# RWKV decays and learning rates: made per unit of 128 tokens, or per block of 512 tokens from split operands and passed through DRAM

## The chip, the cores and the metric

One core of a Trainium2 chip runs the whole kernel. The metric is the device time of one execution in microseconds. The engines are TensorE (PE in the profile, its weight loads PEld), VectorE (DVE), ScalarE (ACT), GpSimd (POOL) and SyncE (SP), which issues every DMA of this kernel, in order. A timed run of the kernel before took 2934.18 us in the median.

## The reference

A decoder layer over 2048 tokens of width 1024: a mixer (gated linear attention, GLA, beside an RWKV-7 group) and a gated MLP. The change concerns two small products of the RWKV group, low-rank ("LoRA") maps from 64 to 512 columns:

```
p = p + (token_shift(p) - p) * mu
w_log = -softplus(-(w0 + tanh(p[..., c0:c1]) @ w_up)) - 0.5
decay = exp(-exp(w_log))
a = sigmoid(a0 + p[..., c1:c2] @ a_up)
k = k * (1 + (a - 1) * k_a)
y = wkv7_scan(r, decay, k, v, -kk, kk * a)
```

Here c0:c1 and c1:c2 are 64 columns each of the projection. The kernel uses sigmoid(z) = (1 + tanh(z/2)) / 2, so the logarithm of the decay is -exp(-0.5) times a sigmoid.

## The kernel before, in words

Tokens are cut into 4 blocks of 512 (NB). `stage_b(b)` projects block b: per 128 output columns 24 products of 128x512 into one PSUM bank (`gemm3`: operands split into a high and a low fp32r part, three products for each of 8 slices of the depth). There are two such banks (`gbank`, tag "g"). `evacuate` empties a bank with ACT, mixes in the token before (DVE, POOL) and stores the result by DMA to DRAM (`pd`); it goes through tiles named ev, a ring of three (`nev`). Column tile TWA holds the 64 decay columns and the 64 rate columns on 128 partitions; it comes before TPG and the 12 tiles of r, k and v.

The weights of the projections (`Weights`) come in pieces of 128x512. In block 0 a piece is loaded into w_st (ring of 4), split into w_hi and w_lo (ring of 6 each, `nhl`) and the two parts are stored to DRAM (khi, klo); later blocks load the parts back.

The recurrences work in units of 128 tokens, 16 in all. For each unit, `rwkv_p` prepares the operands, `rwkv_i` and `rwkv_j` invert a small triangular matrix, `rwkv_s` does the state steps and `gla` the attention chunk. In `rwkv_p` (lines 770 to 808) a unit loads its 128 columns of TWA as rw_wa (L776), takes tanh of the first 64 partitions (L792), makes eight fp32 products of depth 64 into two rp banks (L797 decays, L798 rates), finishes them with tanh on ACT (L800, L803), a scaling on POOL (L801, L805) and the factor of k on DVE (L804), and runs the prefix sum of the log decays (L808).

A list scheduler fixes the order of every engine's instructions when the kernel is built. Between steps of a unit `fill` emits, at a lower priority, the next steps of the projection of the following block: while block b's units run, `stage_b(b+1)` is the filler. `boundary` empties the filler before the first unit of a block is prepared. Block 0's projection is emitted alone, ahead of all units; only the first two GLA chunks overlap with it.

Of the kernel before, what the change touches and what calls it, by code (L numbers as in the profile page):

```python
# [95 lines left out]
def hybrid_kernel(ctx, tc, x, cst, vec, c_row, ada_t, w_in, w_v, w_first, w_z, gk_up, wa_up, g_up,  # L96
# [18 lines left out]
    def gbank():  # L115
        return pools["psum"].tile([P, 512], F32, name="g_bank", tag="g", bufs=pools["g"])
# [11 lines left out]
    def vcol(name, k=0, n=1):  # L128
        o, w = _VL[name]
        return vt[:, o + k:o + k + n]  # L130
# [5 lines left out]


    proj = [[None] * NPROJ for _ in range(NBLK)]
    groups = ((TQ, 2), (TK, 2), (TV, 4), (TG, 4), (TZ, 1), (TR, 4), (TRK, 4), (TRV, 4), (TWA, 1), (TPG, 1))
    pd = [{t0: dram.tile([P, n, NB], F32, name=f"proj_{b}_{t0}") for t0, n in groups} for b in range(NBLK)]  # L140
    mixd = [dram.tile([P, 8, NB], F32, name=f"mix_{b}") for b in range(NBLK)]
    x2d = [dram.tile([P, KT, NB], F32, name=f"x2_{b}") for b in range(NBLK)]

# [11 lines left out]
        return ct[:, o - P:o - P + w]  # L155

    pools["w"] = ph1.enter_context(tc.tile_pool(name="wp1", bufs=2))
    pools["np"], pools["nst"], pools["nhl"], pools["nev"], pools["nx"] = 2, 4, 6, 3, 2
    pools["h"] = ph1.enter_context(tc.tile_pool(name="hp1", bufs=1))
    pools["hb"] = 9  # L160

# [131 lines left out]
    def dst_of(b, t):  # L293
        for t0, n in groups:
            if t0 <= t < t0 + n:
                return pd[b][t0][:, t - t0, :]
# [25 lines left out]
    def stage_a(b, ks):  # L322
# [2 lines left out]
            ahead[b] = (spread(ap, ahead[b]), [])  # L325
        modulate(ap, src, ahead[b][0], 0, ks, ahead[b][1])

    def evacuate(b, t, ps):
        ev = ap.tile([P, NB], F32, name="ev", tag="ev", bufs=pools["nev"])
        if t < TZ:  # L330
            A.activation(out=ev, in_=ps, func=AF.Copy, scale=0.125 if t < TK else 1.0)
        else:

            m = t - TR
            A.activation(out=ev, in_=ps, func=AF.Copy, scale=omu[:, m:m + 1])
            V.scalar_tensor_tensor(out=ev[:, 1:NB], in0=ps[:, 0:NB - 1], scalar=vcol("mu", m), in1=ev[:, 1:NB], op0=ALU.mult, op1=ALU.add)
            G.tensor_tensor(out=ev[:, 0:1], in0=ev[:, 0:1], in1=carry[:, m:m + 1], op=ALU.add)
            A.activation(out=carry[:, m:m + 1], in_=ps[:, NB - 1:NB], func=AF.Copy, scale=vcol("mu", m))
        nc.sync.dma_start(out=dst_of(b, t), in_=ev)

    def values_tok(b, h, i):
# [21 lines left out]
    def stage_b(b):  # L363

        h = ahead.pop(b)[1]
        order = ([TZ] + list(range(8, TZ)) if b == 0 else list(range(8)) + [TZ] + list(range(8, TZ))) + [TWA, TPG] + [TR + i for i in range(12)]
        for i_, t in enumerate(order):
            if b + 1 < NBLK:
                if i_ == len(order) - 15:
                    ahead[b + 1] = stats_a(b + 1)  # L370
                if i_ == len(order) - 11:
                    stats_b(b + 1)
                if i_ == len(order) - 7:
                    stage_a(b + 1, range(0, EXTRA))
                if i_ == len(order) - 2:
                    stage_a(b + 1, range(EXTRA, KT))
            if t == TZ:

                ps = gbank()
                w = Weights(w_z, split=False, cols=KT * 32)  # L380
                for i in range(2):
                    for p_ in range(2):
                        for j in range(4):
                            k = 4 * i + j
                            PE.matmul(out=ps[32 * j:32 * j + 32], lhsT=w.cut(w.st, k * 32, 32), rhs=h[k][p_].bitcast(F32),
                                      start=i == 0 and p_ == 0, stop=i == 1 and p_ == 1)
                ev = ap.tile([P, NB], F32, name="ev", tag="ev", bufs=pools["nev"])
                A.activation(out=ev, in_=ps, func=AF.Identity, bias=vcol("zone"))
                nc.sync.dma_start(out=pd[b][TZ][:, 0, :], in_=ev)
                yield  # L390
                continue
            if TV <= t < TG:
                if (t - TV) % 2 == 0:
                    yield from values_tok(b, h, (t - TV) // 2)
                continue
            if b > 0 and i_ < 2:
                if i_ == 0:
                    bks = pair_gemm(w_in, 0, "in", h, b + 1 < NBLK)
                ps = bks[i_]
            elif b + 1 < NBLK and i_ >= len(order) - 2:  # L400
                if i_ == len(order) - 2:
                    bks = pair_gemm(w_in, t - 1, "in", h, b + 1 < NBLK)
                ps = bks[i_ - len(order) + 2]
            else:
                ps = gbank()
                t_ = t if t < TZ else t - 1
                gemm3(ps, Weights(w_in[t_], key=("in", t_), keep=b + 1 < NBLK), h)
            evacuate(b, t, ps)
            yield

    filler, lag = [None], [370]
    rate, due = [0.85], [0.0]
# [177 lines left out]
    ahead[0] = (rb, h0)  # L590
    nc.sync.dma_start(out=ct, in_=cst[:, P:c0])

    wa_up = cst1([P, 512], "wa_up", wa_up)
    g_up_sb = cst1([P, 512], "g_up_sb", g_up)
    gk_up_sb = cst1([P, 256], "gk_up_sb", gk_up)
    wlev = cst1([P, 1152], "wlev", dt=F32R)
# [173 lines left out]
    def rwkv_p(b, q, n):  # L770
        cs = slice(q * CQ, (q + 1) * CQ)
        K, R = qp("rw_k"), qp("rw_r")
        VV = ctile([P, 4, CQ], F32, name="rw_v", tag="rw_v", bufs=1)
        wa = ctile([P, CQ], F32, name="rw_wa", tag="rw_wa", bufs=1)
        pg = ctile([P, CQ], F32, name="rw_pg", tag="rw_pg", bufs=2)
        nc.sync.dma_start(out=wa, in_=pd[b][TWA][:, 0, cs])  # L776
        nc.sync.dma_start(out=K, in_=pd[b][TRK][:, :, cs])
        nc.sync.dma_start(out=R, in_=pd[b][TR][:, :, cs])
        nc.sync.dma_start(out=VV, in_=pd[b][TRV][:, :, cs])
# [9 lines left out]
        V.scalar_tensor_tensor(out=vc, in0=vm.unsqueeze(2).broadcast_to([P, 8, 64]), scalar=-1.0 / 64.0, in1=pv, op0=ALU.mult, op1=ALU.add)  # L789

        lw, an, kp_ = qp("rw_lw"), qp("rw_an"), qp("rw_kp")
        A.activation(out=wa[0:64], in_=wa[0:64], func=AF.Tanh)  # L792
        psw, psa = bank("rp"), bank("rp")
        pw_ = psw.rearrange("p (j t) -> p j t", j=4)
        pv = psa.rearrange("p (j t) -> p j t", j=4)
        for j in range(4):
            PE.matmul(out=pw_[:, j, :], lhsT=wa_up[0:64, j * P:(j + 1) * P], rhs=wa[0:64, :], start=True, stop=True)  # L797
            PE.matmul(out=pv[:, j, :], lhsT=wa_up[64:128, j * P:(j + 1) * P], rhs=wa[64:128, :], start=True, stop=True)  # L798
        for j in range(4):
            A.activation(out=lw[:, j], in_=pw_[:, j], func=AF.Tanh, scale=0.5, bias=w0h[:, j:j + 1])  # L800
        G.tensor_scalar(out=lw, in0=lw, scalar1=-0.5 * DECAY, scalar2=-0.5 * DECAY, op0=ALU.mult, op1=ALU.add)  # L801
        for j in range(4):
            A.activation(out=an[:, j], in_=pv[:, j], func=AF.Tanh, scale=0.5, bias=a0h[:, j:j + 1])  # L803
            V.tensor_scalar(out=kp_[:, j], in0=an[:, j], scalar1=kah[:, j:j + 1], scalar2=kah[:, 4 + j:5 + j], op0=ALU.mult, op1=ALU.add)  # L804
        G.tensor_scalar(out=an, in0=an, scalar1=-0.5, scalar2=-0.5, op0=ALU.mult, op1=ALU.add)  # L805
        for i in range(2):
            lwc = lw[:, 2 * i:2 * i + 2].rearrange("p j t -> p (j t)")
            V.tensor_tensor_scan(out=lwc, data0=cc("m64"), data1=lwc, initial=0.0, op0=ALU.mult, op1=ALU.add)  # L808
# [762 lines left out]
```

## Time and profile before

| what | value |
|---|---|
| timed runs, median (lowest to highest of 3) | 2934.18 us (2933.49 to 2939.03) |
| profiled execution, its own time | 2927.03 us |
| span of its trace | 2925.2 us |
| PE, DVE, ACT, POOL busy, share of the span | 94%, 71%, 44%, 37% |
| DMA moved | 486.91 MB, 166 GB/s over the span |

Times in the profile are microseconds from the start of the span unless marked ns. A row of a matmul gives the time from its start until its result is out, so successive matmuls overlap: their pace is read from start to start. An fp32 product is recorded as two instructions. The column after "<-" names what ended an engine's idle time.

### The profile page before, as it was taken

The numbers are of one execution on the slowest core, as the hardware profiler recorded it, in microseconds if no ns is written. First come the engines' busy times: TensorE is split into PE (matmuls) and PEld (weight loads), VectorE is DVE, ScalarE is ACT, GpSimd is POOL, SyncE is SP. The second block draws the span as 40 slices with busy tenths as digits, with TensorE's granted clock in tenths as the row PEclk, the third lists the DMA queues.
The fourth block names the chain that finished last, engine by engine and source line by source line (L and its number), as shares of the span: only waits on it lengthen the run. The fifth ranks groups of instructions, "written<-read, shape, count | busy, mean of one in ns | idle before, by whom it ended". The sixth has DMA issues, their size and how long they took to land.

```text
span 2925.2 us, 54728 instructions
## 1 busy us (share of the span) xinstructions
PE 2751.4 (94%) x20296; PEld 2229.9 (76%) x20296; DVE 2085.8 (71%) x4103; ACT 1298.4 (44%) x2721; POOL 1088.3 (37%) x1150
## 2 busy tenths in 40 slices
PE   6989999999999999999779999999997999999998
PEld 5767777877787777778557888888776788888887
DVE  8356977656676667886687685776868786685867
ACT  4444345444444446443354353442534444353443
POOL 5213222312221223332456363553436454363541
PEclk9999999999999999889789999999998999999999
DMA  8989945645545566546314425234564624425243
GB/s 287 352 288 312 280 139 178 191 143 159 171 150 154 163 196 206 164 124 213 120 43 162 141 87 166 87 126 149 185 227 144 209 94 129 138 90 162 88 130 110
DMA packets 363532, 486.91 MB, mean 166 GB/s; under 512 B 80769, under 2 KB 153729, under 8 KB 363265
## 3 DMA queue, kind: packets, MB, share of 16 engines
q1 hardware_dynamic: 363264, 483.41, 51.9%
q8 instruction: 160, 2.62, 0.4%
q14 instruction: 108, 0.88, 0.1%
HBM read 342.77 MB, written 140.51 MB: 165 GB/s over the span
## 4 chain that ended last, share of the span: by engine, by line
PE 69%; DVE 13%; DMA 9%; ACT 3%; issue 3%; POOL 2%; SPq 0%; DVEq 0%; POOLq 0%; ACTq 0%
PE g_bank L1270 9%; PE g_bank L1268 9%; PE g_bank L1269 9%; PE g_bank L1325 5%; PE g_bank L1327 5%; PE g_bank L1326 5%; PE g_bank L281 4%; PE g_bank L283 4%; PE g_bank L282 4%; PE gl_bank L698 1%; DMA rw_k<-proj 1%; DMA acc<-acc 1%; PE g_bank L450 1%; DMA w_st<-in_ada_t 1%; PE g_bank L452 1%
## 5 line engine op out<-in xcount | busy, mean ns | idle before, releaser
L1268 PE MATMUL g_bank<-h_hi,w_hi 128*128 128x512 f32 x1232 | 488.0, 396 | 26.6 <-ACT h_hi L1143 14.8
L1269 PE MATMUL g_bank<-h_lo,w_hi 128*128 128x512 f32 x1232 | 487.3, 396 | 12.7 <-DVE h_lo L1165 6.8
L1270 PE MATMUL g_bank<-h_hi,w_lo 128*128 128x512 f32 x1232 | 479.7, 395 | 9.7 <-POOL w_lo L1144 7.8
L1143 ACT CAST w_hi<-w_st 128x512 fp32r<-128x512 f32 (+1 forms) x396 | 238.6, 607 | 487.4 <-PE g_bank L1326 348.4
L1328 DVE SCALAR_TENSOR_TENSOR acc<-g_bank,mod,acc 128x512 f32<-128x512 f32 (+1 forms) x200 | 144.7, 728 | 249.7 <-PE g_bank L1327 230.7
L1144 POOL TENSOR_TENSOR w_lo<-w_st,w_hi 128x512 fp32r<-128x512 f32 x154 | 219.3, 1425 | 241.7 <-ACT w_hi L1143 237.9
L281 PE MATMUL g_bank<-h_hi,w_hi 128*128 128x512 f32 x736 | 299.0, 406 | 8.0 <-DMA w_hi<-khi 3.8
L1268 PEld LDWEIGHTS g_bank<-h_hi,w_hi 128*128 128x128 f32 x1232 | 235.1, 191 | 81.6 <-ACT h_hi L1143 18.0
L282 PE MATMUL g_bank<-h_lo,w_hi 128*128 128x512 f32 x736 | 294.9, 401 | 0.0
L283 PE MATMUL g_bank<-h_hi,w_lo 128*128 128x512 f32 x736 | 294.9, 401 | 0.0
L1269 PEld LDWEIGHTS g_bank<-h_lo,w_hi 128*128 128x128 f32 x1232 | 235.0, 191 | 64.1 <-DVE h_lo L1165 8.2
L1270 PEld LDWEIGHTS g_bank<-h_hi,w_lo 128*128 128x128 f32 x1232 | 234.9, 191 | 63.3 <-POOL w_lo L1144 12.3
L1325 PE MATMUL g_bank<-hh,w_hi 128*128 128x512 f32 x640 | 251.9, 396 | 6.0 <-DVE acc L1328 6.0
L1326 PE MATMUL g_bank<-hl,w_hi 128*128 128x512 f32 x640 | 251.6, 395 | 0.0
L1327 PE MATMUL g_bank<-hh,w_lo 128*128 128x512 f32 x640 | 251.6, 395 | 0.0
L1144 DVE TENSOR_TENSOR w_lo<-w_st,w_hi 128x512 fp32r<-128x512 f32 (+1 forms) x242 | 201.6, 833 | 15.2 <-ACT w_hi L1143 10.5
L281 PEld LDWEIGHTS g_bank<-h_hi,w_hi 128*128 128x128 f32 x736 | 140.3, 191 | 41.6 <-issue 4.5
L283 PEld LDWEIGHTS g_bank<-h_hi,w_lo 128*128 128x128 f32 x736 | 140.1, 190 | 30.8 <-DMA w_lo<-klo 0.7
L282 PEld LDWEIGHTS g_bank<-h_lo,w_hi 128*128 128x128 f32 x736 | 140.6, 191 | 28.0 <-issue 0.2
L1325 PEld LDWEIGHTS g_bank<-hh,w_hi 128*128 128x128 f32 x640 | 120.1, 188 | 37.3 <-DVE acc L1328 6.9
L1327 PEld LDWEIGHTS g_bank<-hh,w_lo 128*128 128x128 f32 x640 | 120.2, 188 | 29.4
L1326 PEld LDWEIGHTS g_bank<-hl,w_hi 128*128 128x128 f32 x640 | 120.2, 188 | 29.1
(342 smaller groups left out, 6108.7 us busy)
## 6 DMA issues: line engine op xcount, KB each, us to landing
acc<-acc SPq DMA_DIRECT2D x352, 256.0 KB, 3.1
w_hi<-khi SPq DMA_DIRECT2D x188, 256.0 KB, 3.5
w_lo<-klo SPq DMA_DIRECT2D x188, 256.0 KB, 3.8
w_st<-in_ffn_up SPq DMA_DIRECT2D x176, 256.0 KB, 2.9
proj<-ev SPq DMA_DIRECT2D x100, 256.0 KB, 3.5
w_st<-in_ffn_down SPq DMA_DIRECT2D x80, 256.0 KB, 2.7
khi<-w_hi SPq DMA_DIRECT2D x68, 256.0 KB, 3.8
klo<-w_lo SPq DMA_DIRECT2D x68, 256.0 KB, 3.9
```

The source lines that it names most:

```text
L281: PE.matmul(out=ps, lhsT=wh, rhs=hi, start=k == 0, stop=False)
L282: PE.matmul(out=ps, lhsT=wh, rhs=lo, start=False, stop=False)
L283: PE.matmul(out=ps, lhsT=wl, rhs=hi, start=False, stop=k == KT - 1)
L1143: A.copy(out=hi, in_=t)
L1144: eng.tensor_tensor(out=lo, in0=t, in1=hi.bitcast(F32), op=ALU.subtract)
L1268: PE.matmul(out=ps, lhsT=wh[:, c], rhs=hi, start=first and k == 0, stop=False, skip_group_check=True)
L1269: PE.matmul(out=ps, lhsT=wh[:, c], rhs=lo, start=False, stop=False, skip_group_check=True)
L1270: PE.matmul(out=ps, lhsT=wl[:, c], rhs=hi, start=False, stop=last and k == 3, skip_group_check=True)
L1325: PE.matmul(out=ps, lhsT=wh, rhs=hh, start=j == 0, stop=False)
L1326: PE.matmul(out=ps, lhsT=wh, rhs=hl, start=False, stop=False)
L1327: PE.matmul(out=ps, lhsT=wl, rhs=hh, start=False, stop=j == n - 1)
L1328: V.scalar_tensor_tensor(out=a_, in0=ps, scalar=mod[:, 40 + ft:41 + ft], in1=a_, op0=ALU.mult, op1=ALU.add)
```

## The change

The products are moved from the units into the projection of a block. After tile TWA is evacuated (it is no longer stored to DRAM), `lora(b, ev)` takes tanh of the first 64 partitions, splits both halves into a high and a low part, and stacks the two parts of one half on 128 partitions (lo_s0 for the decays, lo_s1 for the rates). The weights are stacked in the same way: the same 64 rows twice, then split into a high and a low matrix (`lora_w`). Two products of 128x512 per 128 output columns, hi and lo weights against the stacked operand, so give all four partial products. Eight banks per block are emptied by ACT's tanh into ev tiles, scaled on POOL (and on DVE for the factor of k, in ev tiles of its own), and stored in 12 DMAs of 256 KB per block to `lod`. A unit then loads its decays, rates and factors of k (three DMAs of 256 KB) into the tiles that it computed before. The rings of w_hi and w_lo have 4 pieces instead of 6.

```
-    groups = (..., (TRV, 4), (TWA, 1), (TPG, 1))
+    groups = (..., (TRV, 4), (TPG, 1))
+    lod = [[dram.tile([P, 4, NB], F32, name=f"lora_{b}_{i}") for i in range(3)] for b in range(NBLK)]
...
-    pools["np"], pools["nst"], pools["nhl"], pools["nev"], pools["nx"] = 2, 4, 6, 3, 2
+    pools["np"], pools["nst"], pools["nhl"], pools["nev"], pools["nx"] = 2, 4, 4, 3, 2
...
+    def lora(b, ev):
+        r0, r1 = slice(0, 64), slice(64, 128)
+        A.activation(out=ev[r0], in_=ev[r0], func=AF.Tanh)
+        both = []
+        for i, (hi, lo) in enumerate(((r0, r1), (r1, r0))):
+            s_ = ap.tile([P, NB], F32R, name=f"lo_s{i}", tag=f"lo_s{i}", bufs=1)
+            A.copy(out=s_[hi], in_=ev[hi])
+            V.tensor_tensor(out=ev[hi], in0=ev[hi], in1=s_[hi].bitcast(F32), op=ALU.subtract)
+            A.copy(out=s_[lo], in_=ev[hi])
+            both.append(s_)
+        for i in range(2):
+            for j in range(4):
+                ps = gbank()
+                for p_ in range(2):
+                    PE.matmul(out=ps, lhsT=lora_w[i][p_][:, j * P:(j + 1) * P], rhs=both[i], start=p_ == 0, stop=p_ == 1)
+                o_ = ap.tile([P, NB], F32, name="ev", tag="ev", bufs=pools["nev"])
+                A.activation(out=o_, in_=ps, func=AF.Tanh, scale=0.5, bias=(w0h, a0h)[i][:, j:j + 1])
+                if i == 1:
+                    k_ = ap.tile([P, NB], F32, name="ev", tag="ev", bufs=pools["nev"])
+                    V.tensor_scalar(out=k_, in0=o_, scalar1=kah[:, j:j + 1], scalar2=kah[:, 4 + j:5 + j], op0=ALU.mult, op1=ALU.add)
+                    nc.sync.dma_start(out=lod[b][2][:, j, :], in_=k_)
+                c_ = (-0.5 * DECAY, -0.5)[i]
+                G.tensor_scalar(out=o_, in0=o_, scalar1=c_, scalar2=c_, op0=ALU.mult, op1=ALU.add)
+                nc.sync.dma_start(out=lod[b][i][:, j, :], in_=o_)
...
-            evacuate(b, t, ps)
+            ev = evacuate(b, t, ps)
             yield
+            if t == TWA:
+                lora(b, ev)
+                yield
...
-        nc.sync.dma_start(out=wa, in_=pd[b][TWA][:, 0, cs])
...
         lw, an, kp_ = qp("rw_lw"), qp("rw_an"), qp("rw_kp")
-        A.activation(out=wa[0:64], in_=wa[0:64], func=AF.Tanh)
-        psw, psa = bank("rp"), bank("rp")
...
-            PE.matmul(out=pw_[:, j, :], lhsT=wa_up[0:64, j * P:(j + 1) * P], rhs=wa[0:64, :], start=True, stop=True)
-            PE.matmul(out=pv[:, j, :], lhsT=wa_up[64:128, j * P:(j + 1) * P], rhs=wa[64:128, :], start=True, stop=True)
...
+        for t_, from_ in zip((lw, an, kp_), lod[b]):
+            nc.sync.dma_start(out=t_, in_=from_[:, :, cs])
```

How the order of instructions moves, at three places. The first is PE in the projection of block 0, where tile TWA (bank 921 before) ends. Before:

```order
L281 MATMUL g_bank_921<-h_hi_567,w_hi_934 128x512
L282 MATMUL g_bank_921<-h_lo_568,w_hi_934 128x512
L283 MATMUL g_bank_921<-h_hi_567,w_lo_935 128x512
L281 MATMUL g_bank_972<-h_hi_217,w_hi_975 128x512
L282 MATMUL g_bank_972<-h_lo_218,w_hi_975 128x512
```

Now, the last four of lora's eight banks there, and the start of the next projection, TPG (bank 1068); gl_vt and atf belong to the first GLA chunk:

```order
L345 MATMUL g_bank_1028<-lo_s1_996,lora_1h_645 128x512
L345 MATMUL g_bank_1028<-lo_s1_996,lora_1l_646 128x512
L345 MATMUL g_bank_1038<-lo_s1_996,lora_1h_645 128x512
L345 MATMUL g_bank_1038<-lo_s1_996,lora_1l_646 128x512
L345 MATMUL g_bank_1048<-lo_s1_996,lora_1h_645 128x512
L345 MATMUL g_bank_1048<-lo_s1_996,lora_1l_646 128x512
L756 MATMUL gl_bank_2933<-gl_vt_2615,atf_678 128x128 x2
L761 MATMUL gl_bank_2938<-gl_vt_2615,gl_kt_2632 64x128 x4
L756 MATMUL gl_bank_2933<-gl_vt_2615,atf_678 128x128 x2
L345 MATMUL g_bank_1058<-lo_s1_996,lora_1h_645 128x512
L345 MATMUL g_bank_1058<-lo_s1_996,lora_1l_646 128x512
L283 MATMUL g_bank_1068<-h_hi_225,w_hi_1071 128x512
```

Before, the next projection follows at once. Now 16 products into eight banks stand between TWA and TPG, and the first GLA chunk's products have moved among them and ahead of them.

The second place is SP's queue at the same point (the stores of lora are L351 and L354, w_st are weights of later projections):

```order
L187 DMA w_st<-in_w_in 128x512
L354 DMA lora_0_107<-ev 128x512 x3
L673 DMA gl_qk<-proj_2_72 128x2x128
L674 DMA gl_qk<-proj_0_71 128x2x128
L354 DMA lora_0_107<-ev 128x512
L351 DMA lora_2_109<-ev 128x512
L354 DMA lora_1_108<-ev 128x512
L832 DMA rw_lw<-lora_0_107 128x4x128
L676 DMA gl_vt<-proj_4_73 128x512
L351 DMA lora_2_109<-ev 128x512
L354 DMA lora_1_108<-ev 128x512
L678 DMA gl_g<-proj_8_74 128x4x128
```

Of these only the loads of weights and of GLA's operands were there before. The first unit's load of its decays (rw_lw) stands between the stores and follows the last store of the decays.

The third place is PE in block 1, where state steps of a unit (rs banks) run beside the projection of the next block. Before:

```order
L283 MATMUL g_bank_4686<-h_hi_1569,w_lo_4689 128x512
L1009 MATMUL rs_bank_3387<-rw_uv_3342,rw_bkt_1970 64x64 x8
L663 MATMUL gl_bank_5077<-wlev_633,gl_gh_5023 128x384 x2
L663 MATMUL gl_bank_5093<-wlev_633,gl_gh_5023 128x384 x2
L281 MATMUL g_bank_4686<-h_hi_1576,w_hi_4691 128x512
L282 MATMUL g_bank_4686<-h_lo_1577,w_hi_4691 128x512
L283 MATMUL g_bank_4686<-h_hi_1576,w_lo_4693 128x512
L924 MATMUL rj_bank_3429<-rw_x32_3424,rw_mab_2357 32x32 x13
L1025 MATMUL rs_bank_3406<-rw_t_1799,rw_sv_3337 64x64 x8
```

Now, around lora's first four banks of that block:

```order
L1052 MATMUL rs_bank_3395<-rw_t_1871,rw_sv_3310 64x64 x8
L1056 MATMUL rs_bank_3395<-rw_rbk_1974,rw_uv_3313 64x64 x8
L345 MATMUL g_bank_4028<-lo_s0_4020,lora_0h_638 128x512
L345 MATMUL g_bank_4028<-lo_s0_4020,lora_0l_639 128x512
L345 MATMUL g_bank_4035<-lo_s0_4020,lora_0h_638 128x512
L345 MATMUL g_bank_4035<-lo_s0_4020,lora_0l_639 128x512
L951 MATMUL rj_bank_3477<-rw_x32_3472,rw_mab_2405 32x32 x12
L1018 MATMUL rs_bank_3413<-rw_sv_3385,rw_t_1871 64x64 x8
L951 MATMUL rj_bank_3477<-rw_x32_3472,rw_mab_2405 32x32 x20
L345 MATMUL g_bank_4042<-lo_s0_4020,lora_0h_638 128x512
L345 MATMUL g_bank_4042<-lo_s0_4020,lora_0l_639 128x512
```

Between two state steps stood products of a projection; now lora's stand there, and no projection follows until its eighth bank is done.

## Rows read from the trace of the kernel before

**Rows 1.** The page's first line.
```profile
span 2925.2 us, 54728 instructions
```

**Rows 2.** One tile, rw_wa: durations min/median/max in ns, first and last start.
```profile
L797 PE MATMUL rp_bank<-rw_wa,wa_up x128: 271/272/374, 228.8 to 1287.7; 64*128 64x128 f32 x128
```

**Rows 3.** Busy us by stretch: length, PE, PEld, DVE, ACT, POOL; PE clock, DMA share, GB/s.
```profile
77.00:180.00 103.00, 102.29 (x585) 82.41 (x585) 44.17 (x100) 53.51 (x114) 24.23 (x37) 1.00 0.95 337
180.00:400.00 220.00, 195.40 (x1802) 160.46 (x1801) 165.53 (x458) 92.59 (x231) 62.64 (x70) 0.93 0.86 275
400.00:800.00 400.00, 385.50 (x4630) 310.95 (x4626) 267.45 (x805) 183.08 (x484) 92.57 (x141) 0.96 0.54 160
800.00:1100.00 300.00, 291.44 (x3442) 235.41 (x3446) 198.71 (x603) 142.65 (x378) 64.04 (x105) 0.98 0.55 170
1100.00:1410.00 310.00, 296.14 (x3370) 237.73 (x3361) 226.58 (x639) 143.10 (x372) 95.38 (x112) 0.92 0.55 171
```

**Rows 4.** Longest waits of PE in 77 to 1410: us in total, times, longest.
```profile
PE g_bank L450 <- ACT carry L338: 12.3, 3, 8.3
PE gl_bank L690 <- ACT atf L704: 5.4, 3, 4.0
```

**Rows 5.** Timeline of PE around one unit's products: start us, us, instruction.
```profile
287.79 1.16 PE L797 MATMUL rp_bank<-rw_wa,wa_up 64*128 64x128 f32 x8
288.87 0.50 PE L282 MATMUL g_bank<-h_lo,w_hi 128*128 128x512 f32 x1
289.21 0.39 PE L283 MATMUL g_bank<-h_hi,w_lo 128*128 128x512 f32 x1
289.44 0.40 PE L281 MATMUL g_bank<-h_hi,w_hi 128*128 128x512 f32 x1
...
293.99 0.39 PE L283 MATMUL g_bank<-h_hi,w_lo 128*128 128x512 f32 x1
294.31 1.16 PE L798 MATMUL rp_bank<-rw_wa,wa_up 64*128 64x128 f32 x8
295.39 0.44 PE L757 MATMUL rp_bank<-ct,rw_kk 128*32 128x8 f32 x32
```

**Rows 6.** Groups by line, ACT: busy us, mean ns of one, idle before and releaser.
```profile
L190 ACT CAST w_hi<-w_st 128x512 fp32r<-128x512 f32 x84 | 50.9, 618 | 33.9 <-DMA w_st<-in_w_in 14.1 <-PE g_bank L282 8.8 <-DMA w_st<-in_w_first 2.9
L335 ACT ACTIVATE ev<-g_bank,omu 128x512 f32<-128x512 f32 x56 | 38.2, 684 | 17.9 <-PE g_bank L283 17.2
...
L803 ACT ACTIVATE rw_an<-rp_bank,a0h 128x128 f32<-128x128 f32 x64 | 18.3, 374 | 17.0 <-PE rp_bank L798 16.9
L800 ACT ACTIVATE rw_lw<-rp_bank,w0h 128x128 f32<-128x128 f32 x64 | 18.3, 372 | 19.8 <-PE rp_bank L797 19.7
...
L792 ACT ACTIVATE rw_wa<-rw_wa 64x128 f32<-64x128 f32 x16 | 5.0, 311 | 16.4 <-DMA rw_wa<-proj 16.3
```

**Rows 7.** Groups by line, DVE and POOL.
```profile
L336 DVE SCALAR_TENSOR_TENSOR ev<-g_bank,vt,ev 128x511 f32<-128x511 f32 x56 | 41.4, 743 | 17.9 <-ACT ev L335 16.0 <-DMA w_hi<-khi 1.6
...
L801 POOL TENSOR_SCALAR rw_lw<-rw_lw 128x512 f32<-128x512 f32 x16 | 10.9, 678 | 48.4 <-ACT rw_lw L800 41.5 <-issue 5.8 <-POOL ev L337 0.9
```

**Rows 8.** DMA issues in 77 to 180: count, KB each, median us to landing.
```profile
proj<-ev SPq DMA_DIRECT2D x15, 256.0 KB, 4.7
```

**Rows 9.** Groups by line, PE: the small products of the recurrences.
```profile
L698 PE MATMUL gl_bank<-gl_d 64*64 64x64 f32 x1280 | 59.3, 233 | 0.0
...
L663 PE MATMUL gl_bank<-wlev,gl_gh 128*128 128x384 f32 x192 | 50.6, 366 | 2.8 <-ACT gl_gh L649 1.9 <-ACT gl_d L664 0.9
...
L991 PE MATMUL rs_bank<-rw_sv,rw_t 128*64 128x64 f32 x512 | 29.5, 238 | 2.3 <-ACT rw_yq L1030 2.3
...
L715 PE MATMUL gl_bank<-gl_vt,atf 128*128 128x128 f32 x128 | 28.0, 307 | 1.5 <-ACT atf L706 1.5
```

**Rows 10.** Busy us in 490 to 500, columns as in rows 3.
```profile
490.00:500.00 10.00, 7.44 (x147) 6.18 (x147) 7.80 (x17) 3.47 (x8) 1.95 (x4) 0.66 0.27 93
```

**Rows 11.** DMA issues in 400 to 800, columns as in rows 8.
```profile
proj<-ev SPq DMA_DIRECT2D x33, 256.0 KB, 3.1
```

**Rows 12.** Longest wait of SP's queue in 77 to 1410: us, times, longest.
```profile
SPq L179 <- PE g_bank L283: 130.0, 72, 12.9
```

More of the change, by code (lines that the diff above doesn't have):

```diff
@@ L138, in hybrid_kernel @@
     proj = [[None] * NPROJ for _ in range(NBLK)]
-    groups = ((TQ, 2), (TK, 2), (TV, 4), (TG, 4), (TZ, 1), (TR, 4), (TRK, 4), (TRV, 4), (TWA, 1), (TPG, 1))
+    groups = ((TQ, 2), (TK, 2), (TV, 4), (TG, 4), (TZ, 1), (TR, 4), (TRK, 4), (TRV, 4), (TPG, 1))
     pd = [{t0: dram.tile([P, n, NB], F32, name=f"proj_{b}_{t0}") for t0, n in groups} for b in range(NBLK)]
+    lod = [[dram.tile([P, 4, NB], F32, name=f"lora_{b}_{i}") for i in range(3)] for b in range(NBLK)]
     mixd = [dram.tile([P, 8, NB], F32, name=f"mix_{b}") for b in range(NBLK)]
@@ L338, in evacuate @@
             A.activation(out=carry[:, m:m + 1], in_=ps[:, NB - 1:NB], func=AF.Copy, scale=vcol("mu", m))
+            if t == TWA:
+                return ev
         nc.sync.dma_start(out=dst_of(b, t), in_=ev)
@@ L407, in stage_b @@
                 gemm3(ps, Weights(w_in[t_], key=("in", t_), keep=b + 1 < NBLK), h)
-            evacuate(b, t, ps)
+            ev = evacuate(b, t, ps)
             yield
+            if t == TWA:
+                lora(b, ev)
+                yield
     filler, lag = [None], [370]
@@ L591, in hybrid_kernel @@
     nc.sync.dma_start(out=ct, in_=cst[:, P:c0])
-    wa_up = cst1([P, 512], "wa_up", wa_up)
+    lora_w = []
+    for i in range(2):
+        t_ = ap.tile([P, NB], F32, name="wtmp", tag="ev", bufs=pools["nev"])
+        for j in range(2):
+            nc.sync.dma_start(out=t_[j * 64:(j + 1) * 64], in_=wa_up[i * 64:(i + 1) * 64])
+        pair = [cst1([P, NB], f"lora_{i}{s_}", dt=F32R) for s_ in "hl"]
+        A.copy(out=pair[0], in_=t_)
+        V.tensor_tensor(out=pair[1], in0=t_, in1=pair[0].bitcast(F32), op=ALU.subtract)
+        lora_w.append(pair)
     g_up_sb = cst1([P, 512], "g_up_sb", g_up)
@@ L773, in rwkv_p @@
         VV = ctile([P, 4, CQ], F32, name="rw_v", tag="rw_v", bufs=1)
-        wa = ctile([P, CQ], F32, name="rw_wa", tag="rw_wa", bufs=1)
         pg = ctile([P, CQ], F32, name="rw_pg", tag="rw_pg", bufs=2)
-        nc.sync.dma_start(out=wa, in_=pd[b][TWA][:, 0, cs])
         nc.sync.dma_start(out=K, in_=pd[b][TRK][:, :, cs])
@@ L791, in rwkv_p @@
         lw, an, kp_ = qp("rw_lw"), qp("rw_an"), qp("rw_kp")
-        A.activation(out=wa[0:64], in_=wa[0:64], func=AF.Tanh)
-        psw, psa = bank("rp"), bank("rp")
-        pw_ = psw.rearrange("p (j t) -> p j t", j=4)
-        pv = psa.rearrange("p (j t) -> p j t", j=4)
-        for j in range(4):
-            PE.matmul(out=pw_[:, j, :], lhsT=wa_up[0:64, j * P:(j + 1) * P], rhs=wa[0:64, :], start=True, stop=True)
-            PE.matmul(out=pv[:, j, :], lhsT=wa_up[64:128, j * P:(j + 1) * P], rhs=wa[64:128, :], start=True, stop=True)
[L799 to L805, printed above, removed]
+        for t_, from_ in zip((lw, an, kp_), lod[b]):
+            nc.sync.dma_start(out=t_, in_=from_[:, :, cs])
         for i in range(2):
```

## The prediction

> **What bounds the kernel now.** I read the page's first line, then busy time by stretch, then what PE waits for, then single instructions. The execution is 2925.2 us long [rows 1]. The products of decays and rates start from 228.8 to 1287.7 us [rows 2], and the tokens' projections that the change touches start at 77, so these stretches matter: the first token block's projections (77 to 180), where PE is busy 102.3 of 103.0 us and the DMA engines 95% of their time; 180 to 400, where PE idles 24.6 of 220 us with DMA at 86%; and the rest of the mixer to 1410, where PE idles 14.5, 8.6 and 13.9 us [rows 3]. So TensorE's own work sets the pace, PE idles 61.6 us in 180 to 1410, and no wait of PE for a decay or rate is among the longest [rows 4]. A removed TensorE microsecond therefore comes back almost whole, and a new TensorE wait is paid almost whole.
>
> **Step 1, products removed.** In a unit the decay's four products come as 8 records: the first starts at 287.79 and the next instruction at 288.87, so 1.08 us. The rates' follow a 128x512 product that starts at 293.99; they start at 294.31 and the next begins at 295.39. A steady 128x512 product takes 0.227 us from start to start (289.21 to 289.44), so the group costs 295.39 - 293.99 - 0.23 = 1.17 us [rows 5]. Sixteen units times 2.25 us: **-36.0 us**, all on PE.
>
> A rule that speaks against the change has to be weighed here. The two groups lie 6.5 us apart [rows 5], with other products between them, and each pays its full price. The Trainium skill (TensorEngine Tiling (Array Packing), Key Properties and When to Use Tiling) says that products over 64 rows should be run as two row tiles, which work in parallel, for up to twice the speed. By that rule the removed pairs would have cost half, and the sum would be 18 us worse; these rows show them apart, so it does not hold here, and it stands below as a rival.
>
> **Step 2, products added.** Four blocks times 16 products of 128x512: 64 x 0.227 = 14.5 us. After a group of another shape the first large product takes 0.34 us instead of 0.23 (288.87 to 289.21) [rows 5]; eight pairs a block, four blocks, 0.11 us each: 3.5 us. Together **+18.0 us**.
>
> **Step 3, the first block's ring.** The results leave through the tiles named ev, three of them, and a tile is free only when its store has landed. Per tile: a write by ACT of 0.684 us (nearest row: the evacuation at L335), a scaling on POOL of 0.678 (L801's shape) [rows 6, 7], and a store that lands after 4.7 us in this stretch [rows 8]: 6.1 us a turn. Lora needs 12 tiles, so four turns. TensorE has two g banks; the next projection can start only when the seventh product's bank has been emptied, into tile 9, in the third turn: 2 x 6.1 + 0.7 = 12.9 us after the first write. Until then the order leaves PE lora's own products (3.6 us) and, of gla, two of four groups of 64x64 products and the output products. A group is 1/64 of 59.3 us, 0.9, and the outputs of a chunk 1/16 of 28.0, 1.8 [rows 9]: 3.6 together. So PE stands for 12.9 - 3.6 - 3.6 = 5.7 us. Ahead of that, evacuation, shift, tanh and three casting steps of 0.6 to 0.75 us [rows 6, 7] make some 4 us, which gla's other pieces fill: eight L663 (8/192 of 50.6 us, 2.1) and two groups (1.9) [rows 9]; I add 1 us. The projection's own evacuation needs the fifth turn at 24.4 us, when PE has run out at 23.8; DVE's extra step on half the tiles makes that 2.5 us. **+9 us**, between 3 (only this last part and a little) and 17 (twice the wait, or TensorE at half clock after it: 490 to 500 shows 2.6 us idle and a clock of 0.66 [rows 10]). SP is held too: the load of rw_lw behind the fourth store waits until that has landed, with weights queued behind; by the order eight weight pieces are fetched before it, which covers four projections.
>
> The Trainium skill (DMA: Bandwidth & Descriptors, Anatomy of one DMA) gives about 2.0 us plus bytes over 436 GB/s for one DMA, 2.6 us for 256 KB. By that the turn is 4.0 us and the stall above 1.5 us instead of 5.7, and the sum 4.2 us better; the stores measured in this stretch take 4.7 [rows 8], and that I use.
>
> **Step 4, the other three blocks.** A store lands in 3.1 us [rows 11], so a turn is 4.5 us and tile 9 comes at 9.7. Here units are in flight: the order puts some six groups of state products between lora's (1/32 of 29.5 us, 0.9 each [rows 9]) and two of gla: 5.5 + 1.9 + 3.6 = 11 us. The bank is no wait by itself. But where a projection's products stood between two state steps before, lora's now do, with bank waits of their own; each state step ends in copies on ACT before the next. Priced as one ACT write (0.684) for six steps, 4 us a block: **+12 us**, from 0 to 20.
>
> **Step 5, chains in the units.** A unit loses tanh (0.31), one group (1.08), four writes (4 x 0.372) and POOL's step (0.68) ahead of the scan, 3.6 us [rows 5, 6, 7]; ACT waited 19.7 and 16.9 us for these products and 16.3 for the load [rows 6]. The new loads (3 x 256 KB a unit instead of 64 KB) stand ready long before, and a DMA at 55% carries them. ACT and DVE lose a little work in sum and POOL gains a little, none of it on PE. Of 61.6 us idle I give back a tenth: **-6 us**, from -12 to 0. The tanh, casts and subtractions moved to the projections cost nothing else; if ACT were the bound there, 8 x 0.684 + 5 x 0.6 = 8.5 us a block would show.
>
> **Step 6, weight buffers 6 to 4.** A projection uses two high and two low pieces, 24 products, 5.4 us. With six buffers a piece is fetched two projections ahead, with four one: 5.4 us against a landing of 3.1. Covered, but SP already waits 130.0 us, up to 12.9 at a time, for TensorE to free them [rows 12], and with that cover gone TensorE waits itself. **+3 us**, from 0 to 12.
>
> **Sum:** -36.0 + 18.0 + 9 + 12 - 6 + 3 = 0. The profiled execution took 2927.03 us, so 2927 by itself; the median of the runs shown, 2934.18, is 7.1 us above it, and there **2934 us**, no change. 0.2% (5.9 us) is about what a measurement of this kernel can tell from no change.
>
> **The rivals.**
> *Faster: the ring hides.* Gla and unit work fill the waits of steps 3 and 4, down to 3 us, and the shorter chains give 10: -36 + 18 + 3 - 10 = -25, 2909 us. For: PE follows a static order in which other work stands between lora's products. Against: in the first block that work is 3.6 us between the first product and the projection.
> *Slower: the ring binds everywhere.* Each turn holds ACT, DVE and SP as well, which execute in order, and PE finds no large product until lora is through: 17 + 20 us, no relief: -36 + 18 + 17 + 20 + 3 = +22, 2956 us. It decides from the point at which the stalls of steps 3 and 4 pass 15 us together (with step 6 and no relief, the zero of the sum). Against: 3.1 us landings in three of four blocks.
> *Slower: four buffers are too few.* A shortfall of 0.25 us at each of 81 projections of the later blocks is 20 us in place of 3: 2951 us. Against: the 2.3 us of cover.
> *Slower: the removed products ran at half price as row tiles:* 2952 us. Against: the 6.5 us between them.
>
> **How the numbers follow.** Chances: forecast 0.45, ring hides 0.27, ring binds 0.15, buffers 0.10, row tiles 0.03. The forecast's own range is -12 to +12 us (2922 to 2946), with 0.28 of it below -5.9 and 0.25 above +5.9. Faster: 0.27 + 0.13 = 0.40; slower: 0.28 + 0.11 = 0.39; within 0.2%: 0.21. As both signs hold much, the range reaches from the first rival to the second: 2909 to 2957.
>
> **What would show it.** Step 1: no L797 or L798, and PE's busy time down by about 36 less 18 us. Step 3: in the first block a gap of PE ahead of a lora product or the next projection, released by ACT's tanh, which itself waits for a landed store of lora; SP waiting at rw_lw. Step 4: the same with up to 2 us each, and PE waiting for ACT's copies between state steps. Step 5: less PE idle in 400 to 1410. Step 6: PE waits for w_hi from its DMA. I am wrong if the first block's stretch grows by under 5 or over 20 us, or if the waits for w_hi pass 12 us.

## The result and the profile after

The change makes the kernel slower: 2968.19 us, median of four runs, against 2935.73 us in the same rounds; ratio 1.0119 (95% interval 1.0098 to 1.0139), some 35 us (the medians differ by 32.5). The forecast was 2934, and the time lies above its range of 2909 to 2957.

The page of the changed kernel, first lines (its execution took 2964.16 us; columns as in [rows 1], then busy us, share and instructions of each engine):

```profile
span 2962.4 us, 54474 instructions
...
PE 2767.9 (93%) x20104; PEld 2222.9 (75%) x20104; DVE 2073.5 (70%) x4065; ACT 1296.3 (44%) x2631; POOL 1079.5 (36%) x1150
```

The span is 37.2 us longer. TensorE was busy 2751.4 of 2925.2 us before, so it is busy 16.5 us more and idle 20.7 us more, though it executes 192 instructions fewer. I had expected it busy about 18 us less.

Busy time by stretch of the changed kernel, the same stretches and columns as [rows 3]:

```profile
77.00:180.00 103.00, 99.29 (x642) 78.43 (x641) 45.76 (x130) 53.96 (x122) 25.97 (x40) 0.92 0.85 299
180.00:400.00 220.00, 195.90 (x1655) 151.60 (x1654) 165.37 (x426) 95.02 (x214) 58.67 (x69) 0.89 0.87 285
400.00:800.00 400.00, 386.61 (x4187) 304.44 (x4189) 259.00 (x748) 168.18 (x412) 91.59 (x135) 0.95 0.60 183
800.00:1100.00 300.00, 285.43 (x3245) 231.13 (x3244) 188.01 (x573) 133.36 (x337) 60.46 (x101) 0.94 0.57 175
1100.00:1410.00 310.00, 284.84 (x3281) 227.78 (x3280) 223.30 (x640) 143.61 (x355) 87.69 (x111) 0.96 0.64 200
```

No single stretch holds the loss. When ACT has emptied the bank of a block's last projection, the changed kernel is 12, 30, 43 and 54 us behind in the four blocks; 17 of these come back later. Idle time alone does not tell it either. TensorE's timeline shows where to look: following the starts of the projections' products one sees four stretches in which none starts, 24, 40, 35 and 32 us long, and lora stands in each. The kernel before has none above 15 us between 77 and 1190. Busy time in these four in the changed kernel, same columns:

```profile
109.20:133.40 24.20, 20.49 (x165) 14.96 (x163) 12.65 (x49) 14.44 (x41) 8.38 (x15) 0.65 0.60 205
361.20:401.70 40.50, 30.93 (x490) 24.16 (x489) 30.18 (x92) 18.01 (x43) 8.47 (x13) 0.60 0.77 251
683.10:718.20 35.10, 29.44 (x304) 22.48 (x303) 25.72 (x79) 25.09 (x53) 13.71 (x19) 0.81 0.45 138
999.90:1031.60 31.70, 28.81 (x323) 22.52 (x322) 27.11 (x86) 21.64 (x48) 9.54 (x17) 0.84 0.48 147
```

and in the kernel before, at the same times:

```profile
109.20:133.40 24.20, 24.16 (x171) 19.95 (x171) 13.62 (x35) 13.34 (x30) 9.10 (x16) 1.00 1.03 381
361.20:401.70 40.50, 37.04 (x491) 30.28 (x489) 31.63 (x87) 21.10 (x49) 11.47 (x20) 1.00 0.61 198
683.10:718.20 35.10, 35.10 (x471) 28.98 (x470) 23.29 (x88) 12.15 (x41) 5.30 (x13) 0.98 0.57 161
999.90:1031.60 31.70, 31.70 (x461) 24.35 (x459) 21.58 (x55) 14.90 (x45) 8.53 (x12) 1.00 0.52 155
```

Two losses stand in the first table. TensorE idles 131.5 - 109.7 = 21.8 us (3.5 before). And its granted clock (PE clock, the share of 2.4 GHz that TensorE was given) falls to 0.65, 0.60, 0.81 and 0.84, so part of each stretch runs at 1.2 instead of 2.4 GHz: busy time times the missing share is 7.2 + 12.4 + 5.6 + 4.6 = 29.8 us (0.7 before). This is an estimate from these rows, and an upper one: it takes every product to be twice as slow at half the clock, and the small ones are not (last section).

The second stretch on TensorE, part of its timeline (start, us, engine, line, operation, names and shapes; in brackets the idle time ahead and what ended it):

```profile
370.30 0.79 PE L345 MATMUL g_bank<-lo_s,lora_0h 128*128 128x512 f32 x1 [1.22 <-ACT lo_s L339]
370.89 0.63 PE L345 MATMUL g_bank<-lo_s,lora_0l 128*128 128x512 f32 x1
371.32 0.63 PE L345 MATMUL g_bank<-lo_s,lora_0h 128*128 128x512 f32 x1
371.75 0.63 PE L345 MATMUL g_bank<-lo_s,lora_0l 128*128 128x512 f32 x1
372.31 0.54 PE L951 MATMUL rj_bank<-rw_x,rw_mab 32*32 32x32 f32 x24
...
376.96 0.69 PE L1026 MATMUL rs_bank<-p1s,yf 128*64 128x64 f32 x16
379.05 0.67 PE L959 MATMUL rj_bank<-rw_z,rw_qm 32*32 32x32 f32 x54 [1.40 <-ACT rw_qm L953]
381.29 1.12 PE L1036 MATMUL rs_bank<-rw_uv,rw_bkt 128*64 128x64 f32 x16 [1.57 <-ACT rw_uv L1029]
...
389.40 1.12 PE L1052 MATMUL rs_bank<-rw_t,rw_sv 64*64 64x64 f32 x16 [3.17 <-DVE rw_sv L1040]
390.45 1.12 PE L1056 MATMUL rs_bank<-rw_rbk,rw_uv 128*64 128x64 f32 x16
```

Lora's products start 0.43 us apart, where a projection's took 0.227 [rows 5]. Between them stand steps of a unit that each wait for the copy of the step before, and nothing large is there to run meanwhile. The Trainium skill (TensorE: Matmul & The Clock Gate, Wait — 56ns, not 53.3ns?) gives 426.7 ns from start to start for 512 columns at 1.2 GHz and 215.7 ns at 2.4; these rows agree with the first and nearly with the second.

### The profile page after: what moved, and what is told of

It is laid out like the page before. It is cut to its first block, busy times and chain, and to the rows that moved or that the text cites. A ratio compares the mean times of both kernels' runs of the same rounds, so it can differ in the third digit from the quotient of the medians.

```text
span 2962.4 us, 54474 instructions
## 1 busy us (share of the span) xinstructions
PE 2767.9 (93%) x20104; PEld 2222.9 (75%) x20104; DVE 2073.5 (70%) x4065; ACT 1296.3 (44%) x2631; POOL 1079.5 (36%) x1150
## 4 chain that ended last, share of the span: by engine, by line
PE 71%; DVE 13%; DMA 9%; ACT 3%; issue 2%; POOL 1%; SPq 0%; DVEq 0%; POOLq 0%; ACTq 0%
PE g_bank L1297 9%; PE g_bank L1295 9%; PE g_bank L1296 9%; PE g_bank L1352 5%; PE g_bank L1354 5%; PE g_bank L1353 5%; PE g_bank L283 4%; PE g_bank L285 4%; PE g_bank L284 4%; PE gl_bank L739 1%; DMA x_k<-in_x 1%; DMA w_st<-in_ada_t 1%; PE gl_bank L704 1%; PE g_bank L415 1%; PE rp_bank L878 1%
## 5 line engine op out<-in xcount | busy, mean ns | idle before, releaser
L1297 PEld LDWEIGHTS g_bank<-h_hi,w_lo 128*128 128x128 f32 x1232 | 234.2, 190 | 59.6 <-POOL w_lo L1171 10.9
```

The source lines that it names most:

```text
L1297: PE.matmul(out=ps, lhsT=wl[:, c], rhs=hi, start=False, stop=last and k == 3, skip_group_check=True)
```

## The experiments

Ratios are to the kernel before in the same rounds; 0.001 is 2.9 us. A difference of two versions carries both intervals, some 7 to 13 us either way.

**Parts of the change alone.** Four weight buffers in the kernel before:

```
-    ..., pools["nhl"], ... = 2, 4, 6, 3, 2
+    ..., pools["nhl"], ... = 2, 4, 4, 3, 2
```

> The kernel before with four weight buffers (w_hi, w_lo) instead of six, nothing else. The cover theory (the eight products of lora, standing as one step, take the projections' products away from between the state steps of the units, so that TensorE idles and falls to 1.2 GHz) gives the buffers little: within 6 us of the kernel before (ratio 0.998 to 1.002). The buffer rival gives 12 to 33 us more (ratio 1.004 to 1.011), with TensorE waiting for w_hi from its DMA.

Measured: 1.0019 (1.0002 to 1.0037), 5.6 us, between 0.6 and 10.9. The buffers are a small cost.

The changed kernel without lora, with the loads:

```
-            if t == TWA:
-                lora(b, ev)
-                yield
...
+    for i, v_ in enumerate((-0.3, -0.5, 1.0)):
...
+            nc.sync.dma_start(out=lod[0][i][:, j, :], in_=o_)
```

> The changed kernel without lora: decays, rates and factors of k are constants, stored once at the start, and each unit loads them as in the change (this leaves the computation of decays and rates out). Four weight buffers. It has the removal and the loads, and none of lora's products, stores or ring. If the removal is worth what I priced (36 us of products and 6 us of shorter chains), the ratio to the kernel before is 0.984 to 0.989; then lora itself costs 65 to 80 us, not 39. If the loads cost time of their own (the rival: a DMA of 256 KB in front of the scan is later than the products were), or the buffers do, the ratio is 0.994 to 1.004 and lora costs 20 to 50 us.

Measured: 0.9901 (0.9862 to 0.9940), between the two cases that I had named. Against four buffers alone it is 1.2%, 35 us, for products removed and loads added. The change itself lies 2.2%, 64 us, above it (some 13 either way), and that is lora. TensorE's line of the page with four buffers alone, then with the loads alone:

```profile
PE 2763.1 (94%) x20296; PEld 2233.3 (76%) x20296; DVE 2074.3 (70%) x4103; ACT 1301.6 (44%) x2721; POOL 1086.7 (37%) x1150
```

```profile
PE 2728.1 (94%) x20040; PEld 2197.5 (76%) x20040; DVE 2065.3 (71%) x4039; ACT 1262.7 (43%) x2577; POOL 1058.3 (36%) x1121
```

TensorE is busy 35.0 us less, the spans (2942.9 and 2906.0) differ by 36.9. From the loads alone to the change it is busy 39.8 us more and idle 16.6 more. The clock moves along: over whole executions, in the mean of its runs, it was 0.961 in the kernel before, 0.958 with four buffers, 0.964 with the loads alone and 0.956 in the change.

**The ring.** Four ev tiles, `pools["nev"]` 3 to 4:

> The changed kernel with four ev tiles instead of three, so that the turn of the ring carries a third more. Ring theory (TensorE stands because ev tiles come free only when a store has landed): the change's 33 us shrink by 12 to 25 us, ratio to the kernel before 1.003 to 1.008, and in the first block the gap before the projection after lora shrinks by at least a third. Cover theory: ratio 1.008 to 1.013, at most 8 us better than the change.

Measured: 1.0097 (1.0073 to 1.0122), 6 us better, which can't be told from none, and the first block's stretch shrinks from 24 to 22 us, not by a third: against the ring theory. No stores of lora (both `dma_start` of `lora` taken out, constants loaded):

> The changed kernel, lora in one piece with all its products, tanh and scalings, but without its twelve stores a block; the units load constants stored at the start (this leaves the computed decays and rates out of the result). An ev tile is then free when POOL has scaled it, not when a store has landed. Ring theory (landings make the cost of one piece): about 18 us of products above the loads alone, ratio to the kernel before 0.996 to 1.002. If the cost lies in the one piece as such (bank waits on ACT, and no large products for TensorE between state steps until it is through): 1.004 to 1.010.

Measured: 1.0098 (1.0067 to 1.0129). With no landing in lora's way, nearly the whole loss stays. Its four stretches without a projection, same columns as above:

```profile
115.00:140.00 25.00, 22.30 (x164) 15.87 (x164) 13.71 (x50) 15.36 (x36) 8.54 (x14) 0.59 0.36 129
358.00:409.00 51.00, 36.88 (x500) 28.61 (x499) 40.47 (x121) 21.32 (x53) 12.29 (x15) 0.57 0.62 192
691.00:722.00 31.00, 27.89 (x291) 22.69 (x290) 25.56 (x71) 24.21 (x51) 11.02 (x19) 0.78 0.35 95
1003.00:1032.00 29.00, 27.53 (x248) 20.16 (x246) 24.91 (x80) 22.16 (x48) 11.34 (x19) 0.88 0.38 103
```

They are as long as the change's and at as low a clock. Six ev tiles, the stacked operands in the ring of x tiles:

```
-            s_ = ap.tile(..., tag=f"lo_s{i}", bufs=1)
+            s_ = ap.tile(..., tag="xt", bufs=pools["nx"])
```

> The changed kernel in one piece with six ev tiles (the two stacked operands moved into the ring of x tiles, which is idle there, to make room). Ring theory: two turns instead of four, so TWA to TPG in the first block falls from 31 us to about 18, and the ratio from 1.012 to 1.000 to 1.005; by the run with four tiles (1.0097) I think half of that likelier: 1.004 to 1.008.

Measured: 1.0030 (1.0008 to 1.0052), 26 us better than the change. But in the first block the stretch only fell from 24 to 21 us; it is the second block's that fell from 40 to 20. So the number of tiles matters, yet hardly through landings. It also changes the order in which the instructions are laid down: in the second block TensorE's timeline has three of lora's banks in a row before a state step, where the change has two. That this order makes the gain is argued, not shown; the stacked operands also sit in another ring here.

**Lora's place.** Pairs behind projections:

```
+        yield
         for i in range(2):
             for j in range(4):
...
+                if (4 * i + j) % 2 == 1:
+                    yield
...
-            if t == TWA:
-                lora(b, ev)
-                yield
+            if t == TWA:
+                left = lora(b, ev)
+            if t >= TR:
+                next(left, None)
+            yield
```

> The changed kernel with lora's eight products not as one step but in pairs, one pair behind each of the next four projections (TPG and three of TR), so the count of steps is that of the kernel before. Cover theory: projections stand between the state steps again, half-clock time in 230 to 420 falls from 53 to under 25 us, and the ratio to the kernel before falls from 1.012 to 0.994 to 1.003. Ring rival: the ring is relieved too (two to four tiles per projection of 5.4 us), so it gives the same here, and is told apart by the four ev tiles. Late-load rival (units wait for decays that come from DRAM): the last store comes later than in the change, so no gain, ratio 1.010 to 1.016.

Measured: 1.0024 (1.0010 to 1.0039), 28 us better than the change with the same three tiles and four buffers. Its longest stretch without a projection is 17 us. The sign set for the clock did not come in its profile: over 230 to 420 us the granted clock is 0.85 in the change and 0.89 with pairs, so half-clock time falls from some 57 to 42 us and not under 25. That execution took 2960.98 us, against a median of 2944.85; in the mean of its ten runs the whole clock is 0.961, as in the kernel before.

> The changed kernel with lora in the same step as tile TWA's projection (the yield between them is taken out), so the place between state steps that lora took is given back to a whole projection, and lora's sixteen products still stand in one run. Cover theory in its narrow form (a state step lost its projection because lora was counted as one): the ratio to the kernel before falls from 1.012 to 1.002 to 1.006. If instead the run of eight bank waits itself, wherever it stands, makes the cost: 1.009 to 1.014, as in the change, and only pairs help.

Measured: 1.0145 (1.0109 to 1.0180). The narrow form falls: a projection more in place of lora's own step gives nothing. The next projection still stands behind all sixteen products.

> Lora in one piece in the first block, as in the change, and in pairs behind projections in the other three. If the later blocks make the cost (step 4 of the prediction), this is within 6 us of pairs in all blocks (2945; ratio 1.001 to 1.005). If the first block's ring makes it (step 3), it stays at 1.008 to 1.012.

Measured: 1.0082 (1.0062 to 1.0103), between the two. Against pairs everywhere the first block's single piece costs 17 us; against the change, pairs in the other three gain 11, little more than the intervals allow. Neither place has it all.

All products behind TPG (the yield of the pairs only after the operands and after the eighth bank):

> The changed kernel, three ev tiles, the operands of lora made behind TWA as before, but all sixteen products in one piece behind the next projection, TPG, so that the chain that makes the operands is covered by 24 products. If that chain makes the cost: 1.002 to 1.006. If the run through two banks in one piece makes it: 1.009 to 1.014. Half of each: 1.006 to 1.009.

Measured: 1.0085 (1.0055 to 1.0114), 10 us better than the change, hardly more than the intervals allow. The chain that makes the operands can be worth that much at most; in the change PE itself, its weight loads (PEld) apart, waits little for it (idle time ahead of line 345, us and times), and for lora's banks not at all:

```profile
  ACT lo_s L339: 2.8, 2
```

25 us over the kernel before remain with the run in one piece, and here not by the clock: the runs behind TPG were granted 0.962 in the mean, as much as the kernel before.

**Other banks, more tiles, less to store.** Single products into the units' banks (`ps = bank("rp")`, a yield after each):

> One product of lora behind each of the eight projections after TWA, into the units' rp banks instead of the projections' g banks, so that no projection waits for lora's bank and none of lora's for a projection's evacuation. If bank waits between projections and lora are what is left of the cost in pairs: 5 to 15 us better than pairs (ratio 0.997 to 1.000). If the units' chains are held at the rp banks instead: 1.004 to 1.012.

Measured: 1.0045 (1.0017 to 1.0073), in the range for units that are held, but not to be told from pairs: one stretch of 43 us without a projection stands at 364.

> Pairs in all blocks and four ev tiles. If what is left of the ring costs something in pairs too, 4 to 8 us better than pairs alone (ratio 0.999 to 1.001); if the ring is no matter once the products are spread, the same as pairs (1.001 to 1.004).

Measured: 0.9985 (0.9966 to 1.0004), no difference from the kernel before that can be told.

> Pairs with six ev tiles. Pairs with three gave 1.0024, with four 0.9985. If the ring still binds at four: 0.993 to 0.997. If four are enough: 0.997 to 1.000.

Measured: 1.0071 (1.0044 to 1.0098), against both cases. (As with six tiles above, the stacked operands are in the ring of x tiles.) And the factor of k made in the units from the loaded rates, pairs and four tiles:

```
+        for j in range(4):
+            V.tensor_scalar(out=kp_[:, j], in0=an[:, j], scalar1=kah[:, j:j + 1], scalar2=kah[:, 4 + j:5 + j], ...)
```

> Pairs with four ev tiles, and the factor of k is made in the units from the loaded rates (four small DVE steps a unit, as before the change) and neither stored nor loaded: eight ev tiles and eight stores a block instead of twelve, two loads a unit instead of three. If ring and DMA still cost something: 0.993 to 0.997. If the unit's DVE steps cost as much as they save: 0.997 to 1.001.

Measured: 1.0109 (1.0081 to 1.0136), against both too. Its last unit ends 38 us after that of pairs with four tiles, though its projections ended only 8 us later. Which steps make the difference there was not found.

**The order itself.** Edits that should only relieve the kernel came out slower, so an edit without work of its own was tried, `lag = [None], [370]` to 360 or 380, in both kernels:

> The kernel before with a lag of 360 instead of 370 for the filler work: no instruction more or less, another order on each engine. If the order matters little: 0.998 to 1.002. If an order is worth 10 us and more, and the lag of the kernel before is at a good one: 1.003 to 1.010.

> The kernel before with a lag of 380. As for 360: 0.998 to 1.002 if the order matters little, 1.003 to 1.010 if it matters and 370 is a good draw.

> The changed kernel with a lag of 360. If its 33 us are its own: 1.010 to 1.014. If a large part is a poor order: anywhere from 1.002 to 1.018, and the mean over lags is what the change costs.

> The changed kernel with a lag of 380. As for 360: 1.010 to 1.014 if the 33 us are its own, 1.002 to 1.018 if the order decides.

Measured: the kernel before 0.9975 (0.9960 to 0.9989) and 0.9999 (0.9984 to 1.0014); the changed one 1.0111 (1.0096 to 1.0126) and 1.0106 (1.0086 to 1.0126). Each against the kernel before at the same lag, the change costs 31 to 40 us in three orders, so the loss is its own. And the best version at another lag:

> Pairs and four ev tiles (0.9985 at a lag of 370) with a lag of 360. If the version beats the kernel before by itself: 0.995 to 0.999. If 0.9985 was a good draw of the order: 0.999 to 1.004.

Measured: 1.0030 (1.0011 to 1.0050). So 0.9985 was in part a good order; no version was found that beats the kernel before by itself.

These runs side by side, with the stretches without a projection (us, from TensorE's timelines) and the granted clock of whole executions (mean of each version's runs):

```
                          stretches at lora      clock   ratio
change                    24, 40, 35, 32         0.956   1.0119
change, lag 360           22, 41, 35, 34         0.955   1.0111
change, lag 380           24, 41, 37, 35         0.953   1.0106
no own step               24, 40, 35, 30         0.955   1.0145
no stores                 25, 51, 31, 29         0.956   1.0098
four ev tiles             22, 29, 30, 33         0.955   1.0097
behind TPG                20, 28, 28, 27         0.962   1.0085
first block in one piece  24, then 15 at most    0.956   1.0082
six ev tiles              21, 20, 33, 31         0.958   1.0030
singles, units' banks     43 at most             0.955   1.0045
pairs                     17 at most             0.961   1.0024
pairs, four tiles         18 at most             0.961   0.9985
pairs, four, lag 360      12 at most             0.961   1.0030
pairs, six tiles          15 at most             0.956   1.0071
pairs, four, k in units   17 at most             0.955   1.0109
```

Long stretches go with long times, but not one for one. The last two rows have no long stretch, and one of them loses as much as the change, so a stretch without projections is not the only thing that costs. The clock goes with the time more often: at 0.956 and below every version loses 13 us or more, at 0.961 and above all but the one behind TPG lie within 9 us of the kernel before. No run changes the clock alone, so what is cause and what effect there is not shown.

## Why the prediction was wrong

**Step 1's price holds; that it comes back whole is not shown.** The removed products were priced at 36.0 us. Their 256 records in the kernel before last 272 ns in the median (L797 in [rows 2], L798 alike) and fill 37.0 us from start to next start. The Trainium skill's rule on row tiles (TensorEngine Tiling (Array Packing), When to Use Tiling) would have made it 18; these rows speak for the full price, as the forecast took it. TensorE is busy 35.0 us less without them, but not by them alone: with the clock of the runs up from 0.958 to 0.964, 0.0058 x 2763 = 16 us of it can be the clock (an estimate from the runs, at most).

**Steps 2 and 4 fail: the clock had no term.** The three steps of lora, 2 to 4, were priced at 18 + 9 + 12 = 39 us; they measured 64 (some 13 either way). Step 2 took 0.227 us a product, the duration at 2.4 GHz; in the change the 64 products take 27.7 us from start to next start instead of 18 (the excess is part of the clock's loss below). Step 4 saw the right mechanism, lora's products in the place of those that covered the state steps, and priced only ACT's copies. In its three stretches TensorE idles 9.6 + 5.7 + 2.9 = 18.2 us against 12, within its bounds, and loses up to another 22.6 us by the clock, for which the step had no term. All four stretches together lose 21.8 idle and up to 29.8 by the clock; less the 4.2 that stand there before, and with 18 us of products, that is 65. That this lies so near 64 is luck: by the clocks of the whole runs, 0.964 with the loads alone and 0.956 in the change, the clock's part is 0.0085 x 2768 = 24 us (estimated the same way). Against the kernel before (0.961) it is 14 us; the profiled execution was idle 20.7 us more.

**Step 3 had the size, not the reason.** In the first block the time from TWA's evacuation to that of the last projection (starts of ACT's line 335, now 363) grew from 98.8 to 110.6 us, 11.8; products and step 3 foresaw 13.5. But the stall is 3.7 us idle and up to 7.2 by the clock. PE's waits in that stretch (us in total, times, longest):

```profile
PE g_bank L283 <- ACT ev L347: 1.4, 1, 1.4
PE gl_bank L113 <- ACT gl_d L705: 1.0, 1, 1.0
PE gl_bank L704 <- ACT gl_d L705: 0.7, 1, 0.7
PE gl_bank L731 <- ACT gl_d L705: 0.6, 1, 0.6
```

The first is the wait that step 3 named, ahead of the next projection, at 1.4 us where it had 5.7. The others are GLA's products ahead of lora, waiting for copies of ACT, which makes lora's operands between them; I thought that time filled. Landings count for little: the stores land faster than in [rows 8] (issues in 77 to 180, columns as there)

```profile
lora<-ev SPq DMA_DIRECT2D x12, 256.0 KB, 2.9
```

and without them nearly the whole loss stays. The Trainium skill (DMA: Bandwidth & Descriptors, Anatomy of one DMA) would give an estimate of 2.6 us, but by a fit that the page states for DMAs issued by GpSimd; the forecast weighed it for SP's without saying so.

**Step 5 did not come.** TensorE's idle time fell by 1.9 us with the loads alone, not by 6. "Stand ready long before" was wrong: DVE's scan, which the loads feed, waits for them (changed kernel, idle time of DVE ahead of what uses rw_lw):

```profile
  DMA rw_lw<-lora: 15.5, 9
```

and with constants stored at the start it waits 16.1 us, ten times. So it is not lora that makes the load late; its own landing and its place in SP's queue are left, and no run separates them.

**Step 6** was priced at 3 us and measured 5.6 (0.6 to 10.9). TensorE's wait for w_hi from its DMA rose from 3.8 to 5.4 us with the four buffers alone and 6.9 in the change.

The sum by the runs: 5.6 - 34.6 + 64 = 35, against 3 - 42 + 39 = 0. The first two terms erred by 10 us, inside what the runs can tell apart; lora erred by 25.

The rival that ended nearest was "the ring binds everywhere", 2956 us with 0.15: TensorE finds no large product until lora is through. That observation was right, and its cause, landings in the ring, was not. Of the signs set, TensorE's busy time spoke, up 16.5 us instead of down 18; the two that were to show me wrong did not: the first block grew by 11.8 us, between 5 and 20, and the waits for w_hi stayed under 12. Neither looks at the clock, the term that was missing.

**Open:** why six ev tiles help one piece by 26 us when taking the stores out helps by 6, and why pairs with six tiles, or with the factor of k in the units, lose 25 to 36 us against pairs with four; and what the loss behind TPG is made of, with the clock as before. A new order alone moved times by 7 us at most in the kernel before, 4 in the changed one and 13 in the pairs.

## What to carry to other kernels

Here large products covered chains of small dependent ones, and sixteen products in one piece took their place. That was paid twice: as idle time, and in most versions as a lower clock for what runs there. So give the granted clock of such a place a term and a sign of its own, and price a product that is to stand there at its 1.2 GHz duration as the upper bound. Small groups between the large products beat the change in five versions of six; the sixth lost as much as the change. Before crediting an edit of a scheduled kernel with 10 us, try it under two or three orders.

## What was not expected of the hardware

The clock fell without a long wait. In the changed kernel at the start of lora in the first block TensorE is busy without a gap, and yet at half its clock (columns as above):

```profile
109.40:117.90 8.50, 6.14 (x71) 4.90 (x69) 6.18 (x18) 6.52 (x14) 4.17 (x7) 0.75 0.87 312
117.90:125.00 7.10, 7.10 (x68) 5.21 (x67) 2.79 (x16) 3.09 (x9) 1.86 (x3) 0.50 0.31 113
```

Ahead of it stand 8.5 us of a GLA chunk's small products, with 2.4 us of idle time in pieces of 1.0 us at most; the clock fell within that row. The Trainium skill (TensorE: Matmul & The Clock Gate, A second HAM failure mode: psum-queue depth-cycling) tells of a kernel whose frequent small gaps between groups made the clock swing between its levels. These rows show small gaps ahead of a fall too; that the gaps brought it, and not the kind of products, no run here separates.

And half the clock is not half the speed for everything. A group of 16 products of 64x64 started 1.05 us before the next group in the second stretch, at a clock of 0.50 (389.40 to 390.45 in its timeline), and 0.61 us before it where the clock was 1.00:

```profile
447.46 0.68 PE L1052 MATMUL rs_bank<-rw_t,rw_sv 64*64 64x64 f32 x16
448.07 0.69 PE L1056 MATMUL rs_bank<-rw_rbk,rw_uv 128*64 128x64 f32 x16
```

That is 1.7 times as long, where lora's 128x512 products took 0.43 instead of 0.227 us, 1.9 times.
